# Two constants loaded later, other PSUM banks for the first SwiGLU block, another order of outputs and splits in the S5 layer

## Chip, cores and metric

The kernel runs on one core of a Trainium2 chip. The metric is the device time of one launch, in microseconds (us). Three runs of the kernel before gave 1011.68, 1011.71 and 1012.67 us, median 1011.71. One further run was made with the hardware profiler on: it took 1011.32 us, and its trace spans 1009.5 us from the first instruction to the last. Engine names are those of the profile: PE is TensorE's matmul, PEld its weight load, DVE is VectorE, ACT is ScalarE, POOL is GpSimd, SP is SyncE, whose queue issues most DMAs.

## The reference

A trunk of two layers for 256 tokens of width 1024, all in float32. Each layer adds to the residual `h` half of a SwiGLU of the normalized `h`, then a mixer, then half of a second SwiGLU.

```python
def swiglu(h, w_gate, w_up, w_down):
    return (jax.nn.silu(h @ w_gate) * (h @ w_up)) @ w_down
...
    for layer in range(DEPTH):
        h = h + MACARON_WEIGHT * swiglu(rms_norm(h, ffn_norm[layer, 0]), ffn_w_gate[layer, 0],
                                        ffn_w_up[layer, 0], ffn_w_down[layer, 0])
        hn = rms_norm(h, mix_norm[layer])
...
            h = h + s5_mixer(hn, ...)      # layer 0
            h = h + moba_mixer(hn, ...)    # layer 1
        h = h + MACARON_WEIGHT * swiglu(rms_norm(h, ffn_norm[layer, 1]), ...)
```

The S5 mixer multiplies by `w_in`, runs a diagonal complex state space along the tokens, takes `gelu`, gates with `g * sigmoid(g @ w_glu)` and multiplies by `w_out`. The hidden width of a SwiGLU is 2816.

## The kernel before

**Stages.** Six stages follow one another: f00 (first SwiGLU), s5, f01, f10, moba, f11. The tokens are two tiles t = 0, 1 of 128 rows; `h` stays in SBUF. Nearly every product is made three times as exact as one pass by splitting both operands into a high and a low part: `mm3` issues high x high, high x low and low x high into one PSUM accumulation.

**Weights.** The weights come through one stream (`Stream`, L36). A unit is one DMA'd tile `raw` of 1 MB; there are RAW = 3 such tiles, so the DMA of unit n is issued once unit n - 3 has been split. A unit has two halves. `split` (L72) makes the next half: ACT writes its high part `whi` (L81, or L87 as two pieces where a norm's gain `gT` is multiplied in), DVE writes the low part `wlo` (L82 or L88). There are HB = 9 slots for split halves; `release` gives a slot back after the last matmul on it. Splits are issued in the order of the units, at hand-placed calls of `st.pump()`; what a `pump` finds no slot or no raw tile for is left to a later one, and `get` splits on the spot what is still missing. Since ACT and DVE work in the order in which they were given their instructions, the place of a `pump` decides what stands ahead of a split and behind it.

**PSUM.** Eight banks: two taken in turn by `psM` (products of gate and up, L131), two in turn by `psR` (transposes and small products, L134), four by `psA(i)` (accumulators, L137).

**Start and f00.** ACT's queue issues the identity (L236), the SwiGLUs' norm scales (L252), the mixers' norm scales (L254) and, in `gains` (L274), the mask and the rotary tables; SP's queue issues the first half of x, then the first weights. PE multiplies ones by ones meanwhile (`busy`, L1317). `gains` transposes the scales (L276, L277). `pre` and `parts` bring x into transposed high and low parts, in the `psA` banks. `gu0` (L438) then computes the first block of 256 hidden columns for both token tiles at once, in two `psM` banks; `gated` (L457) takes silu on ACT (L459) into `sg`, issues a pump, and multiplies on DVE (L463). Then comes `gu(1, 0)`, which takes the next `psM` bank. While f00 runs, a generator (`tables`, called from `fill`, L1295) works off the S5 tables; `slot[0]` counts estimated us.

**S5.** `w_in` makes U. For each of 8 blocks b: `t1` (L961) on PE, `rot` (L970) with two scans on DVE and four multiplications on POOL that give `hr`, `y_out` (L1016) with 12 groups of small matmuls into a `psR` bank, gelu on ACT and two transposes `gs` on DVE, `g_tr` (L1036) through another `psR` bank into high and low parts (L1045 on ACT, L1046 on DVE), and `glu` (L1048), 24 matmuls into the four `psA` banks. L1098 to L1103 is the loop for b = 3 to 7: `glu(b-3)`, `y_out(b)`, `t1rot(b+3)`, `g_tr(b-1)`. With the last `glu`, `gate` (L1069) takes a sigmoid on ACT, and on DVE a product (L1074), a cast (L1076) and a difference (L1077) for each pair of blocks; `so` (L1079) multiplies by `w_out`. Pumps stand in `glu` (L1064), and in the loop of `so` over b = 0, 1 and t (L1119, L1120).

**After S5.** `boundary` (L354) does the last two `so` units bank by bank: `finish` (L352, DVE) updates `h`, `prep` (L304) transposes it for the next stage. `ffn_w` (L513) is f01: `gu` with a block of hidden columns on the partitions (L531 to L533), `act` and `dn`.

Of the kernel before, what the change touches and what calls it, by code (L numbers as in the profile page):

```python
# [10 lines left out]
F32 = mybir.dt.float32  # L11
# [104 lines left out]
def trunk_kernel(ctx: ExitStack, tc, x, ffn_norm, ffn_w_gate, ffn_w_up, ffn_w_down, mix_norm,  # L116
                 s5_w_in, s5_a_re, s5_a_im, s5_log_dt, s5_b_re, s5_b_im, s5_c_re, s5_c_im, s5_d,
                 s5_w_glu, s5_w_out, moba_w_qkv, moba_q_norm, moba_k_norm, moba_w_out,
                 consts, out, phases=("f00", "s5", "f01", "f10", "moba", "f11")):
    nc = tc.nc  # L120
    ctx.enter_context(tc.manual_schedule())
    cp = ctx.enter_context(tc.tile_pool(name="const", bufs=1))
# [4 lines left out]
    fp = ctx.enter_context(tc.tile_pool(name="ffn", bufs=2))  # L127
# [3 lines left out]
    def psM():  # L131
        return pp.tile([128, 512], F32, name="pM", tag="M", bufs=2)

    def psR():  # L134
        return pp.tile([128, 512], F32, name="pR", tag="R", bufs=2)

    def psA(i):  # L137
        return pp.tile([128, 512], F32, name=f"pA{i}", tag=f"A{i}", bufs=1)
# [92 lines left out]
    cst = cp.tile([128, 320], F32, name="cst")  # L231
    ident = cst[:, 0:128]
# [1 line left out]
    cosT = cst[:, 256:288].rearrange("p (t f) -> p t f", t=2)  # L234
    sinT = cst[:, 288:320].rearrange("p (t f) -> p t f", t=2)
    nc.scalar.dma_start(ident, consts[:, 0:128])  # L236
    gn = cp.tile([48, 128], F32, name="gn")
    h2 = cp.tile([128, 2, D], F32, name="h2")
    h = [h2[:, t, :] for t in range(2)]

# [5 lines left out]
    def ld_x(n):  # L246
        for s in range(4):
            off, ap = rows(None, s, n)
            nc.sync.dma_start(h2[s * 32:s * 32 + 32, :, n * 512:(n + 1) * 512],
                              bass.AP(tensor=x.tensor, offset=x.offset + off, ap=ap))  # L250

    nc.scalar.dma_start(gn[0:32], ffn_norm.rearrange("l i (k p) -> (l i k) p", p=128))  # L252
    ld_x(0)
    nc.scalar.dma_start(gn[32:48], mix_norm.rearrange("l (k p) -> (l k) p", p=128))  # L254
    warm(AF.Exp)
    ahead.append(lambda: ld_x(1))
    if "s5" in phases:
# [10 lines left out]
    st = Stream(nc, units, rp, hp)  # L268

    gT = cp.tile([128, 48], F32, name="gT")  # L270
    st.gT = gT

    def gains():
        nc.scalar.dma_start(cst[:, 128:320], consts[:, 128:320])  # L274
        ps = psR()
        nc.tensor.transpose(ps[:, 0:48], gn, ident[0:48, 0:48])  # L276
        nc.vector.tensor_copy(gT, ps[:, 0:48])  # L277


    X = {}  # L280
# [131 lines left out]


    def ffn(tag, nxt, hooks, fill):

        V = nc.vector
        acc = [None] * 4
        AT, AC = {}, {}

        def gu(j, t, hooks):  # L420
            us = [where[tag, "g", j, a] for a in range(2)]
            ps = psM()
            ts = slice(t * 128, t * 128 + 128)
            for k in range(8):
                for fn in hooks.get(k, ()):
                    fn()
                fill(0.7)
                wh, wl = st.get(us[k // 4], (k % 4) // 2)
                c = slice((k % 2) * 512, (k % 2) * 512 + 512)
                mm3(ps, X["h"][:, k, ts], X["l"][:, k, ts], wh[:, c], wl[:, c], k == 0, k == 7)  # L430
                if k % 2:
                    if k < 7 and (j, t, k) != (L, 1, 5):
                        st.pump()
                    if t == 1:
                        st.release(us[k // 4], (k % 4) // 2)
            gated(j, t, ps)

        def gu0():  # L438

            us = [where[tag, "g", 0, a] for a in range(2)]  # L440
            pt = [psM() for t in range(2)]
            for q in range(4):
                u = us[q // 2]
                for t in range(2):
                    for f in hooks.get((q, t), ()):
                        f()
                    ts = slice(t * 128, t * 128 + 128)
                    for k in (2 * q, 2 * q + 1):
                        fill(0.7)
                        wh, wl = st.get(u, q % 2)  # L450
                        c = slice((k % 2) * 512, (k % 2) * 512 + 512)
                        mm3(pt[t], X["h"][:, k, ts], X["l"][:, k, ts], wh[:, c], wl[:, c], k == 0, k == 7)
                st.release(u, q % 2)
            for t in range(2):
                gated(0, t, pt[t])

        def gated(j, t, ps):  # L457
            sg = fp.tile([128, 256], F32, name="sg", bufs=1)
            nc.scalar.activation(sg, ps[:, 0:256], AF.Silu, scale=Rr[t])  # L459
            if (j, t) != (L, 1):  # L460
                st.pump()
            AC[t] = fp.tile([128, 256], F32, name="act", bufs=2)
            V.scalar_tensor_tensor(AC[t], ps[:, 256:512], Rr[t], sg, op0=OP.mult, op1=OP.mult)  # L463

        def tr(j, t):
            if t == 0:
                AT[j] = []
                for i, n in enumerate(("ah", "al")):
                    o = AO[2 * i + j % 2]
                    a2 = fp.tile([128, 640], F32R, name=n, bufs=2)  # L470
                    AT[j].append(a2[:, o:o + 512].rearrange("p (f c) -> p f c", c=256))
            ps = psR()
            pv = ps[:, 0:256].rearrange("p (f c) -> p f c", c=128)
            a = AC.pop(t)
            for f in range(2):
                nc.tensor.transpose(pv[:, f, :], a[:, f * 128:(f + 1) * 128], ident)
            ah, al = (x[:, :, t * 128:t * 128 + 128] for x in AT[j])
            nc.scalar.activation(ah, pv, AF.Copy)
            V.tensor_tensor(al, pv, ah.bitcast(F32), op=OP.subtract)

        def dn(j, f):
            u = where[tag, "d", j]
            for t in range(2):
                for n in range(2):
                    if j == 0 and f == 0:
                        acc[2 * t + n] = psA(2 * t + n)
                    bank_mm(acc, t, n, *AT[j], u, [f], j == 0 and f == 0, False)
                    fill(0.7)
                if t == 1:
                    st.release(u, f)  # L490
                st.pump()

        L = NJ - 1
        for j in range(NJ):
            if j == 0:
                gu0()
                continue
            gu(j, 0, {3: [lambda: tr(0, 0)], 6: [lambda: tr(0, 1)]} if j == 1 else {6: [lambda: tr(j - 1, 1)]})
            if j > 1:
                dn(j - 2, 1)  # L500
            gu(j, 1, {6: [lambda: tr(j, 0)]})
            if j:
                dn(j - 1, 0)

        def part(j, f):
            return lambda t, n: bank_mm(acc, t, n, *AT[j], where[tag, "d", j], [f], False, (j, f) == (L, 1))

        boundary(nxt, [part(L - 1, 1), part(L, 0), part(L, 1)], acc, 0.5, lambda: tr(L, 1))
        st.release(where[tag, "d", L - 1], 1)
        for i in range(2):  # L510
            st.release(where[tag, "d", L], i)
# [429 lines left out]
    def s5(nxt, entry):  # L941
# [65 lines left out]
        def t1rot(b):  # L1007
            t1ld(b)
            rot_ld(b)
# [38 lines left out]
        def glu(b, after=None):  # L1048

            u = where["glu", b // 2]  # L1050
            if b == 0:
                for i in range(4):
                    acc[i] = psA(i)
            gh, gl = GT["h"][:, b, :], GT["l"][:, b, :]
            wh, wl = st.get(u, b % 2)
            for o in range(8):
                d = acc[o // 2][:, (o % 2) * 256:(o % 2) * 256 + 256]
                c = slice(o * 128, o * 128 + 128)
                mm(d, wh[:, c], gh, start=b == 0 and o % 2 == 0, stop=False, skip_group_check=True)
                mm(d, wh[:, c], gl, start=False, stop=False, skip_group_check=True)  # L1060
                mm(d, wl[:, c], gh, start=False, stop=b == NB - 1, skip_group_check=True)
                if o == 7:
                    st.release(u, b % 2)
                if o == 3 and b < 7 or o == 7 and b in (5, 6):  # L1064
                    st.pump()
                if after is not None and o % 2 == 1:
                    after(o // 2)
# [28 lines left out]
        t1rot(5)  # L1096
        g_tr(1)
        for b in range(3, NB):  # L1098
            glu(b - 3)
            y_out(b)  # L1100
            if b + 3 < NB:
                t1rot(b + 3)
            g_tr(b - 1)  # L1103
# [8 lines left out]
        for b in range(2):  # L1112
            for t in range(2):
                for n in range(2):
                    so(b, t, n)
                if t == 1:
                    for i in range(2):
                        st.release(where["so", b], i)
                st.pump()  # L1119
            st.pump()  # L1120

        boundary(nxt, [lambda t, n: so(2, t, n), lambda t, n: so(3, t, n, True)], acc, 1.0)
        for b in (2, 3):
# [160 lines left out]
    tab = tables(tabp) if "s5" in phases else iter(())  # L1284
    next(tab, None)
    slot = [0]

    def clock():
        return slot[0]
# [5 lines left out]
    def fill(dt):  # L1295
        slot[0] += dt
        if slot[0] > 9.0:
            next(tab, None)

    def pre(t, n):  # L1300

# [120 lines left out]
```

## Time and profile before

| | us |
|---|---|
| median of 3 runs | 1011.71 |
| profiled run, its own time | 1011.32 |
| span of its trace | 1009.5 |
| f00 ends, s5 starts (first L378 on the s5 weights) | about 226 |
| s5 ends, f01 starts (first L531) | 334.82 |
| DVE busy over the span | 707.0 |
| ACT busy over the span | 574.4 |

A row of the timeline has the start in us, the duration in us, the engine, the source line, the operation, the tiles written and read, and in brackets how long the engine had been idle and what ended that. Matmuls are pipelined, so a record is longer than the distance to the next one. In the table by windows each engine has its busy us and its count of instructions, then follow the TensorE clock that was granted (1.00 is full), the share of the DMA engines and their GB/s. The list of waits names who waited for whom, the us in total, how often, and the longest.

### The profile page before, as it was taken

The numbers are of one execution on the slowest core, as the hardware profiler recorded it, in microseconds if no ns is written. First come the engines' busy times: TensorE is split into PE (matmuls) and PEld (weight loads), VectorE is DVE, ScalarE is ACT, GpSimd is POOL, SyncE is SP. The second block draws the span as 40 slices with busy tenths as digits, with TensorE's granted clock in tenths as the row PEclk, the third lists the DMA queues.
The fourth block names the chain that finished last, engine by engine and source line by source line (L and its number), as shares of the span: only waits on it lengthen the run. The fifth ranks groups of instructions, "written<-read, shape, count | busy, mean of one in ns | idle before, by whom it ended". The sixth has DMA issues, their size and how long they took to land.

```text
span 1009.5 us, 16571 instructions
## 1 busy us (share of the span) xinstructions
PE 993.0 (98%) x6393; PEld 889.0 (88%) x6393; DVE 707.0 (70%) x1144; ACT 574.4 (57%) x1040; POOL 167.3 (17%) x330
## 2 busy tenths in 40 slices
PE   8999999999999999999999999999999999999998
PEld 6788888888997889999989999999888899999997
DVE  4799676857967677666657766666689667766662
ACT  5656778744335656555546555553788655555551
POOL 4981222113740100000000000000342010000000
PEclk9999999999999999999999999999999999999999
DMA  8886776876735467565626665645354456656531
GB/s 258 231 271 225 240 255 216 280 294 234 269 117 196 139 211 248 168 208 168 208 84 209 235 222 169 208 168 172 117 164 139 159 173 210 223 195 208 169 126 42
DMA packets 137535, 197.59 MB, mean 196 GB/s; under 512 B 16288, under 2 KB 109040, under 8 KB 137200
## 3 DMA queue, kind: packets, MB, share of 16 engines
q1 hardware_dynamic: 133088, 183.16, 54.6%
q0 software_dynamic: 3616, 12.66, 3.2%
q8 instruction: 50, 0.82, 0.3%
q10 hardware_dynamic: 752, 0.71, 0.3%
q14 instruction: 29, 0.24, 0.1%
HBM read 182.84 MB, written 13.66 MB: 195 GB/s over the span
## 4 chain that ended last, share of the span: by engine, by line
PE 87%; DVE 5%; issue 3%; POOL 2%; ACT 2%; ACTq 0%; POOLq 0%; DVEq 0%
PE pM L533 12%; PE pM L531 12%; PE pM L532 12%; PE pA L379 9%; PE pA L380 9%; PE pA L378 9%; PE pM L378 5%; PE pM L379 5%; PE pM L380 5%; DVE wlo L82 1%; PE pR L314 1%; POOL qrs L287 1%; PE pR L863 1%; DVE zo L992 1%; PE pR L843 1%
## 5 line engine op out<-in xcount | busy, mean ns | idle before, releaser
L531 PE MATMUL pM<-xa,whi 128*128 128x256 f32 x1056 | 295.7, 280 | 1.9 <-ACT whi L87 1.9
L533 PE MATMUL pM<-xa,wlo 128*128 128x256 f32 x1056 | 294.8, 279 | 0.3 <-DVE wlo L88 0.3
L532 PE MATMUL pM<-xa,whi 128*128 128x256 f32 x1056 | 294.8, 279 | 0.0
L88 DVE SCALAR_TENSOR_TENSOR wlo<-raw,gT,whi 128x512 fp32r<-128x512 f32 x328 | 228.0, 747 | 71.2 <-ACT whi L87 71.1
L82 DVE TENSOR_TENSOR wlo<-raw,whi 128x1024 fp32r<-128x1024 f32 x156 | 193.0, 1252 | 57.5 <-ACT whi L81 56.2
L87 ACT ACTIVATE whi<-raw,gT 128x512 fp32r<-128x512 f32 x328 | 213.5, 711 | 19.1 <-PE pA L380 14.1
L531 PEld LDWEIGHTS pM<-xa,whi 128*128 128x128 f32 x1056 | 198.5, 188 | 4.4 <-ACT whi L87 2.1
L532 PEld LDWEIGHTS pM<-xa,whi 128*128 128x128 f32 x1056 | 198.5, 188 | 2.5
L533 PEld LDWEIGHTS pM<-xa,wlo 128*128 128x128 f32 x1056 | 198.5, 188 | 0.5 <-DVE wlo L88 0.5
L81 ACT ACTIVATE whi<-raw 128x1024 fp32r<-128x1024 f32 x156 | 160.9, 1054 | 21.1 <-DMA raw<-in_ffn_w_up_dram 6.1
L378 PE MATMUL pA<-whi,ah 128*128 128x512 f32 x352 | 138.9, 395 | 0.3 <-ACT whi L81 0.3
L379 PE MATMUL pA<-wlo,ah 128*128 128x512 f32 x352 | 137.8, 391 | 0.8 <-DVE wlo L82 0.8
L380 PE MATMUL pA<-whi,al 128*128 128x512 f32 x352 | 137.7, 391 | 0.0
L378 PE MATMUL pM<-whi,xa 128*128 128x512 f32 x304 | 126.5, 416 | 2.3 <-DVE act L463 1.9
L546 ACT ACTIVATE sg<-gr 128x256 f32<-128x256 f32 x66 | 27.6, 418 | 165.4 <-DVE gr L543 165.4
L379 PE MATMUL pM<-wlo,xa 128*128 128x512 f32 x304 | 119.8, 394 | 1.7 <-DVE wlo L82 1.6
L380 PE MATMUL pM<-whi,xa 128*128 128x512 f32 x304 | 119.7, 394 | 0.0
L329 POOL TENSOR_TENSOR ms<-ss 128x1 f32<-128x1 f32 x10 | 1.9, 194 | 479.5 <-ACT sq L326 479.5
L380 PEld LDWEIGHTS pA<-whi,al 128*128 128x128 f32 x352 | 66.1, 188 | 14.3
L379 PEld LDWEIGHTS pA<-wlo,ah 128*128 128x128 f32 x352 | 66.2, 188 | 12.4 <-DVE wlo L82 1.1
L378 PEld LDWEIGHTS pA<-whi,ah 128*128 128x128 f32 x352 | 66.1, 188 | 12.0 <-ACT whi L81 0.5
L543 DVE TENSOR_TENSOR gr<-pM,rrow 128x512 f32<-128x512 f32 x66 | 45.5, 689 | 39.8 <-PE pM L533 39.7
(248 smaller groups left out, 1264.1 us busy)
## 6 DMA issues: line engine op xcount, KB each, us to landing
raw<-in_ffn_w_down_dram SPq DMA_DIRECT2D x44, 1024.0 KB, 5.1
raw<-in_ffn_w_gate_dram SPq DMA_DIRECT2D x80, 512.0 KB, 3.7
raw<-in_ffn_w_up_dram SPq DMA_DIRECT2D x80, 512.0 KB, 4.9
raw<-in_moba_w_qkv_dram SPq DMA_DIRECT2D x12, 1024.0 KB, 5.1
TB<-dB SPq DMA_DIRECT2D x8, 768.0 KB, 6.4
raw<-in_ffn_w_gate_dram SPq DMA_DIRECT2D x16, 256.0 KB, 4.5
raw<-in_ffn_w_up_dram SPq DMA_DIRECT2D x16, 256.0 KB, 4.7
dB<-tt POOLq DMA_DIRECT2D x16, 256.0 KB, 5.1
```

Source lines behind the costliest of these rows:

```text
L81: nc.scalar.activation(hi, r, AF.Copy)
L82: nc.vector.tensor_tensor(lo, r, hi.bitcast(F32), op=OP.subtract)
L87: nc.scalar.activation(hi[:, c], r[:, c], AF.Identity, scale=g)
L88: nc.vector.scalar_tensor_tensor(lo[:, c], r[:, c], g, hi[:, c].bitcast(F32), op0=OP.mult, op1=OP.subtract)
L378: mm(o, xh, wh, start=start, stop=False)
L379: mm(o, xh, wl, start=False, stop=False)
L380: mm(o, xl, wh, start=False, stop=stop)
L531: mm(o, a, xh, start=k == 0 and i == 0, stop=False, skip_group_check=True)
L532: mm(o, a, xl, start=False, stop=False, skip_group_check=True)
L533: mm(o, b, xh, start=False, stop=k == 7, skip_group_check=True)
L543: V.tensor_tensor(gr, ps.rearrange("p (i c) -> p i c", i=2), Rr["row"][:, None, :].to_broadcast([128, 2, 256]), op=OP.mult)
L546: nc.scalar.activation(sg, gr[:, 0, :], AF.Silu)
```

## The change

- The mixers' norm scales and the second part of the constants (mask, rotary tables) are no longer loaded by ACT's queue at the start. `more_loads` issues both on SP's queue when the count of us passes 30, `more_gains` transposes the mixers' scales when it passes 50. The first transpose has 32 columns and waits for two loads only.
- `gu0` accumulates in `psA(0)` and `psA(2)`. Its two `gated` issue no pump; two pumps follow both. `sg` of f00 takes the two buffers of `gr` in place of one of its own.
- In the S5 loop `y_out(b)` stands ahead of `glu(b-3)`.
- The additional pump at the end of a `glu` stands in blocks 3, 4 and 5, where it stood in 5 and 6. Each t of the `so` loop pumps twice, eight in all; there were six.

```diff
-    nc.scalar.dma_start(gn[0:32], ffn_norm.rearrange("l i (k p) -> (l i k) p", p=128))
+    nc.scalar.dma_start(gn, ffn_norm.rearrange("l i (k p) -> (l i k) p", p=128))
     ld_x(0)
-    nc.scalar.dma_start(gn[32:48], mix_norm.rearrange("l (k p) -> (l k) p", p=128))
...
     def gains():
-        nc.scalar.dma_start(cst[:, 128:320], consts[:, 128:320])
         ps = psR()
-        nc.tensor.transpose(ps[:, 0:48], gn, ident[0:48, 0:48])
-        nc.vector.tensor_copy(gT, ps[:, 0:48])
+        nc.tensor.transpose(ps[:, 0:32], gn, ident[0:32, 0:32])
+        nc.vector.tensor_copy(gT[:, 0:32], ps[:, 0:32])
+
+    def more_loads():
+        nc.sync.dma_start(gm2, mix_norm.rearrange("l (k p) -> (l k) p", p=128))
+        nc.sync.dma_start(cst[:, 128:320], consts[:, 128:320])
+
+    def more_gains():
+        ps = psR()
+        nc.tensor.transpose(ps[:, 0:16], gm2, ident[0:16, 0:16])
+        nc.vector.tensor_copy(gT[:, 32:48], ps[:, 0:16])
...
-            pt = [psM() for t in range(2)]
+            pt = [psA(2 * t) for t in range(2)]
...
-                gated(0, t, pt[t])
-
-        def gated(j, t, ps):
-            sg = fp.tile([128, 256], F32, name="sg", bufs=1)
+                gated(0, t, pt[t], 0)
+            st.pump(2)
+
+        def gated(j, t, ps, pumps=1):
+            sg = fp.tile([128, 512], F32, name="sg", tag="gr", bufs=2)[:, 0:256]
             nc.scalar.activation(sg, ps[:, 0:256], AF.Silu, scale=Rr[t])
             if (j, t) != (L, 1):
-                st.pump()
+                st.pump(pumps)
...
-                if o == 3 and b < 7 or o == 7 and b in (5, 6):
+                if o == 3 and b < 7 or o == 7 and b in (3, 4, 5):
                     st.pump()
...
         for b in range(3, NB):
+            y_out(b)
             glu(b - 3)
-            y_out(b)
...
-                st.pump()
-            st.pump()
+                st.pump(2)
...
+    extra = [(30.0, more_loads), (50.0, more_gains)]
...
         if slot[0] > 9.0:
             next(tab, None)
+        while extra and slot[0] > extra[0][0]:
+            extra.pop(0)[1]()
```

More of the change, by code (lines that the diff above doesn't have):

```diff
@@ L236, in trunk_kernel @@
     nc.scalar.dma_start(ident, consts[:, 0:128])
-    gn = cp.tile([48, 128], F32, name="gn")
+    gn = cp.tile([32, 128], F32, name="gn")
+    gm2 = cp.tile([16, 128], F32, name="gm2")
     h2 = cp.tile([128, 2, D], F32, name="h2")
```

## Prediction

> **What bounds the kernel now.** First the page: the busy shares and the chain that ended last.
>
> ```profile
> PE 993.0 (98%) x6393; PEld 889.0 (88%) x6393; DVE 707.0 (70%) x1144; ACT 574.4 (57%) x1040; POOL 167.3 (17%) x330
> ...
> PE 87%; DVE 5%; issue 3%; POOL 2%; ACT 2%; ACTq 0%; POOLq 0%; DVEq 0%
> ```
>
> PE sets the time. The change removes no matmul, so it can gain only where PE stands still or runs slowly, and the list of PE's waits says where that is.
>
> ```profile
> PE pM L378 <- DVE act L463: 1.9, 1, 1.9
> PE pM L531 <- ACT whi L87: 1.9, 1, 1.9
> ...
> PE pA L379 <- DVE wlo L82: 1.1, 2, 0.8
> PE pA L378 <- DVE xa L1076: 1.0, 1, 1.0
> ```
>
> Each is one or two events of a microsecond or two, and the diff touches what stands around all four. So I took the timeline around each of them, and the order in which the changed program gives each engine its instructions. Idle time in a row understates a stall, since records overlap: I count the distance from one matmul's start to the next, less the usual pace.
>
> **The first block, 24 to 34 us.**
>
> ```profile
> 23.77 1.05 ACT L81 ACTIVATE whi<-raw 128x1024 fp32r<-128x1024 f32 x1
> 24.28 0.40 PE L380 MATMUL pM<-whi,xa 128*128 128x512 f32 x1
> 24.85 1.23 DVE L82 TENSOR_TENSOR wlo<-raw,whi 128x1024 fp32r<-128x1024 f32 x1 [1.82 <-ACT whi L81]
> 26.00 0.47 DVE L463 SCALAR_TENSOR_TENSOR act<-pM,rr,sg 128x256 f32<-128x256 f32 x1
> 26.59 0.47 ACT L459 ACTIVATE sg<-pM,rr 128x256 f32<-128x256 f32 x1 [1.77 <-DVE act L463]
> 26.62 0.47 PE L378 MATMUL pM<-whi,xa 128*128 128x512 f32 x1 [1.94 <-DVE act L463]
> 26.93 0.46 PE L379 MATMUL pM<-wlo,xa 128*128 128x512 f32 x1
> ```
>
> PE ends `gu0` at 24.28 and goes on at 26.62: the bank for `gu(1,0)` is freed by `act`, which stands on DVE behind the split that `gated` had pumped. In the changed program the bank is free. But `gu(1,0)` needs that very split, and it now stands behind both `sg`. The second `sg` cannot start before PE's last product is done (24.28 + 0.40), so about 24.7; it ends at 25.2, `whi` at 26.2, `wlo` at 27.45. PE's first matmul comes at 26.25 rather than 26.62, but the second, which reads `wlo`, at 27.5 rather than 26.93. So the wait is not removed, it is exchanged for one that ends 0.55 us **later**. The clock must be looked at too:
>
> ```profile
> 20.28:23.69 3.41, 3.41 (x16) 2.54 (x15) 1.29 (x3) 1.30 (x3) 2.83 (x11) 1.00 0.67 201
> 23.69:27.10 3.41, 1.47 (x7) 0.94 (x6) 1.62 (x2) 1.64 (x4) 2.81 (x8) 1.00 1.08 252
> 27.10:30.50 3.40, 3.40 (x9) 2.21 (x9) 2.46 (x3) 1.85 (x2) 3.01 (x6) 0.50 0.07 9
> ...
> 337.68:341.10 3.42, 2.00 (x14) 1.80 (x15) 2.89 (x5) 3.42 (x7) 2.75 (x10) 1.00 0.00 0
> ```
>
> After a stretch in which PE was busy for 1.47 of 3.41 us, the clock was half for 3.4 us (9 matmuls in place of 15 or 16, worth up to 1.6 us). In the changed kernel PE is idle from 24.5 to 26.25 and from 26.5 to 27.5, as much as before, so I expect the half clock again. Partly it hides: the later splits follow at 28.7 and 30.0, and PE at half pace meets neither. I take **+0.3**, with bounds of +0.6 (the delay alone) and -1.0 (the delay, and 1.6 gained by full clock).
>
> That `gu0` writes into the banks of `pre` costs nothing: `parts` reads them on DVE ahead of the first `wlo`, for which PE waits anyway. `sg` in two buffers takes away a wait of ACT for DVE, which is not on PE's path here.
>
> The Trainium skill ("TensorE: Matmul & The Clock Gate", section "Why this matters for your kernels") says that throughput doesn't drop as long as PE has no idle gap over about 3 us. The trace disagrees: a gap of 1.94 us was followed by half clock. By the page the changed kernel would keep full clock, and the term would be -1.0.
>
> **The loads at the start.**
>
> ```profile
> 0.98 5.49 PE L1321 MATMUL pR<-ones 128*128 128x128 f32 x24 [0.98 <-POOL ones L224]
> ...
> 6.40 0.34 PE L276 MATMUL pR<-cst,gn 48*128 48x48 f32 x1
> ```
>
> The first transpose follows directly upon the filler (0.98 + 5.49 = 6.47), so PE wouldn't use earlier scales. The first weights may land earlier, as their issues wait for fewer loads, but what follows runs from PE through `pre` and `parts`, not from a DMA. I count 0 (bounds -0.4 and +0.2). The scales' second transpose costs PE a slot like the row at 6.40: **+0.2**. SP issues two more loads, of 8 and 96 KB, ahead of one refill of f00; refills are issued units ahead: 0, at worst +0.5.
>
> **`y_out` ahead of `glu`.**
>
> ```profile
> 267.25 0.36 PE L1059 MATMUL pA<-xa,whi 128*128 128x256 f32 x1
> ...
> 268.12 0.38 DVE L1046 TENSOR_TENSOR xa<-pR,xa 128x256 fp32r<-128x256 f32 x1
> ...
> 268.55 0.38 PE L1060 MATMUL pA<-xa,whi 128*128 128x256 f32 x1 [0.94 <-DVE xa L1046]
> ```
>
> `glu(0)` does one matmul and then waits for the low part of block 0, until 268.55. It looks as if `y_out(3)` could fill that. But it writes into a `psR` bank, and of the two, `g_tr(1)` has just taken one; the other is that of `g_tr(0)`, which is free only when L1046 has read it. So `y_out(3)` waits for the same instruction: gain 0, and the matmul of 267.25 no longer runs in the gap, **+0.1**. The rest of the loop is the same work in another order.
>
> **The pumps at the gate.**
>
> ```profile
> 306.09 1.99 ACT L81 ACTIVATE whi<-raw 128x1024 fp32r<-128x1024 f32 x2
> 307.16 2.36 DVE L82 TENSOR_TENSOR wlo<-raw,whi 128x1024 fp32r<-128x1024 f32 x2 [1.82 <-ACT whi L81]
> 309.31 0.28 PE L1060 MATMUL pA<-xa,whi 128*128 128x256 f32 x1
> 309.44 0.68 DVE L1074 TENSOR_TENSOR gf<-gf,sg 128x512 f32<-128x512 f32 x1
> 310.73 0.47 PE L378 MATMUL pA<-whi,xa 128*128 128x512 f32 x1 [1.02 <-DVE xa L1076]
> ```
>
> The gate's product waits on DVE behind two splits; PE, done at about 309.55, waits for it. With the pump of block 6 gone, one split is left; the product can start at 307.16 + 1.23 = 308.4, and everything behind it comes 1.04 earlier. Less the 0.1 above: **-0.9**. In all there is one pump more ahead of the gate (10 for 9), so both halves of `so(1)` are split before it. That takes away this stall:
>
> ```profile
> 317.21 0.39 PE L378 MATMUL pA<-whi,xa 128*128 128x512 f32 x1
> 317.92 0.37 SPq L170 DMA_DIRECT2D raw<-in_ffn_w_gate_dram  x1
> 317.94 0.50 PE L379 MATMUL pA<-wlo,xa 128*128 128x512 f32 x1 [0.35 <-DVE wlo L82]
> ...
> 321.50 1.34 ACT L87 ACTIVATE whi<-raw,gT 128x512 fp32r<-128x512 f32 x2 [4.16 <-DMA raw<-in_ffn_w_up_dram]
> ...
> 326.89 0.69 DVE L352 SCALAR_TENSOR_TENSOR h<-pA,h 128x512 f32<-128x512 f32 x1 [3.13 <-PE pA L380]
> ```
>
> 317.94 - 317.21 less a pace of 0.23: **-0.5**. The same split freed the raw tile for f01's first weights: their DMA was issued at 317.92, now at about 308.4.
>
> **The eight pumps of `so`.** They make, ahead of the boundary, the last four halves of `so` and four of f01; before it was five and one. That pays here:
>
> ```profile
> 336.31 0.60 PE L314 MATMUL pR<-cst,h 128*128 128x128 f32 x4
> ...
> 338.81 0.38 PE L531 MATMUL pM<-xa,whi 128*128 128x256 f32 x1 [1.91 <-ACT whi L87]
> ...
> 339.60 0.38 PE L533 MATMUL pM<-xa,wlo 128*128 128x256 f32 x1 [0.29 <-DVE wlo L88]
> ...
> 355.21 0.28 PE L533 MATMUL pM<-xa,wlo 128*128 128x256 f32 x1
> 355.75 0.50 PE L378 MATMUL pA<-whi,ah 128*128 128x512 f32 x1 [0.26 <-ACT whi L81]
> 357.01 0.50 PE L379 MATMUL pA<-wlo,ah 128*128 128x512 f32 x1 [0.76 <-DVE wlo L82]
> ```
>
> With the first block's four halves ready, PE goes on after the transposes of 336.31: 2.50 to 338.81, less about 0.4 for them, and 0.4 round 339.60: **-2.5**. ACT and DVE then have two halves fewer to make, and the halves of `dn(0,0)` stand right behind the first `sg` of f01, ready some 4 us ahead of PE. So the pair of stalls at 355 goes: 0.42 + 1.03 = **-1.45**.
>
> What is late next: the last two of f01's halves need its second unit, whose DMA goes out when the second split after the gate is done, about 318.1. The row at 321.50 came 3.6 us after its DMA; so 321.7 for the one and, with a microsecond more of issues, 322.7 for the other; split on DVE by 325.9. `finish` is due at 326.89 - 1.4 = 325.5, behind them on DVE: 0.4 late, and its transposes a full bank's matmuls later: 0 (bound +1).
>
> **Sum**: +0.3 + 0.2 - 0.9 - 0.5 - 2.5 - 1.45 = -4.85, so 4.9 faster. From the profiled run's own 1011.32 (span 1009.5 and 1.8 around it, which I leave as it is) that is 1006.5. The median of the runs is 0.4 above the profiled run, so the forecast is 1006.8 to 1006.9; I put **1006.8**, own range 1005.8 to 1008. The bounds of the single terms added up would give 1003 to 1009; they won't all fall to one side.
>
> **Rivals.**
>
> 1. The boundary holds the gain back. ACT and DVE take their work in order; if f01's second unit lands late, `finish` waits behind its splits, and PE behind `finish`. Against it: the row at 321.50 leaves room. For it: four loads instead of two are in flight, and nothing in the trace shows them at that place. Each us of delay beyond 0.5 is a us lost; with 3 us the time is **1009.3**.
> 2. Full clock in the first block: at 337.68 a stretch with PE busy for 2.00 of 3.42 us kept it, at 23.69 one with 1.47 lost it, and where such stretches begin may shift from run to run. That is 1.3 more than the forecast, **1005.5**. Or `y_out(3)` does fill the gap (if the bank were free): 1.2 more, about the same. Against it: PE is idle for 2.75 of 3 us, and two banks are two.
> 3. Slower: the S5 loop falls behind. `y_out(7)` moves ahead of `glu(4)` and needs `hr(7)` from POOL.
>
> ```profile
> 291.59 1.72 POOL L999 TENSOR_TENSOR hr<-pv,pv 128x256 f32<-128x256 f32 x1
> ...
> 294.90 0.36 PE L1059 MATMUL pA<-xa,whi 128*128 128x256 f32 x1
> ```
>
> `hr(7)` ends at 293.31 and PE comes for it at 294.9: 1.6 us of slack. DVE is nearly full from 268 on, and the changed order puts gelu's transposes ahead of the splits. If each of the four turns from block 3 to block 7 took DVE and POOL t us longer, PE would lose 4t - 1.6; from t = 1.6 on that is more than the 4.85. At t = 2.2 it is 7.2: 1006.8 + 7.2 = **1014**. Against it: the same instructions as before.
> 4. The gain is given back in f01: PE waits again for halves that ACT and DVE cannot make faster. Both have idle time there, and before there is hardly a PE wait behind 357: with most of the 3.95 us of that stage gone, about **1010.5**.
>
> **Chances.** Forecast 0.62; rival 1 0.16, a third of it under 2 us of gain; rival 2 0.14; rival 3 0.05; rival 4 0.03. A measurement tells about 0.2% (2 us) from no change: faster 0.87, same 0.08, slower 0.05. The range from 1004.8 to 1009.2 takes in rival 2 and most of rival 1.
>
> **What would show it.** In the trace after (starts as before unless PE has gained or lost by then): PE's second matmul of `gu(1,0)` waits for `wlo` to about 27.5, with half clock behind it; `y_out(3)` starts only when the low part of block 0 is read out, near 268.5; the gate's stall shrinks from 1.2 to 0.2; no wait of L531 or of the first `dn` in f01; the first load of f01 near 308. Wrong it would be if f01's halves came later than the boundary, or PE waited in blocks 4 to 7 of S5.

## The result and the profile after

The changed kernel took 1009.04 us (median of 9 runs, 1005.99 to 1012.03); the kernel before, run beside it, 1012.67 (9 runs, 1011.41 to 1014.65). The ratio is 0.9958 with a 95% interval of 0.9941 to 0.9976, so some 4.2 us faster (3.6 by the medians) where 4.9 had been forecast.

The runs of the changed kernel fall into two groups, and the granted clock tells them apart: four took 1005.99 to 1006.29 us at a mean clock of 0.999 to 1.000, five took 1009.04 to 1012.03 us at 0.993 to 0.996. The profiled run, 1010.79 us with a span of 1009.0, is of the second kind. So its trace shows what the change gains and also what takes most of it away again. A mean clock of 0.994 over 1009 us stands for some 12 us at half clock; in the trace they are 3.4 us in the first block, 6.8 in S5 and 1.8 at the end, after PE's last matmuls.

From the page of the changed kernel, the busy shares, the chain, and then, from its list of PE's waits (who waits for whom, us in total, times, longest), the rows that matter here:

```profile
PE 996.0 (99%) x6394; PEld 892.6 (88%) x6394; DVE 704.6 (70%) x1145; ACT 574.8 (57%) x1040; POOL 165.3 (16%) x330
...
PE 91%; DVE 3%; issue 2%; POOL 2%; ACT 1%; DMA 0%; SPq 0%; ACTq 0%; POOLq 0%; DVEq 0%
```

```profile
PE pA L387 <- DVE wlo L82: 1.6, 2, 0.8
PE pM L386 <- ACT whi L81: 1.5, 1, 1.5
PE pR L1033 <- issue: 1.1, 1, 1.1
...
PE pM L387 <- DVE wlo L82: 0.9, 2, 0.8
PE pR L322 <- DVE h L360: 0.7, 1, 0.7
```

The lines stand some 9 further down than in the kernel before. All four waits with which the prediction began are gone: `gu(1,0)` for `act`, f01 for `whi`, `so` for the gate's product, `so(1)` and `dn` for `wlo`. (The first row above has the name of the last of them, but it is `gu0`'s own two waits at 11.31 and 18.79 us, which stood under `pM` before `gu0` changed its banks.) In the place of the first stands a wait for `whi` and `wlo`; and there are two new ones: `y_out(3)` (L1033) and the first transposes of the boundary (L322), which wait for `finish`. The 0.9 us for which `glu(0)` waited before are gone too; the wait of `y_out(3)` stands in their place. PE is busy for 3 us more than before, though it does the same work but for one small transpose: its mean clock was 0.994, against 0.998 in the trace of before.

The same matmul in both traces, start before and start after, gives the balance stage by stage:

| matmul | before | after | difference |
|---|---|---|---|
| second product of `gu(1,0)` | 26.93 | 27.46 | +0.53 |
| `act`'s first pair of transposes, the second | 30.54 | 31.09 | +0.55 |
| after the added transpose of the scales | 70.54 | 71.51 | +0.97 |
| `y_out(2)`, first | 262.47 | 263.46 | +0.99 |
| `g_tr(7)`, first | 300.48 | 304.95 | +4.47 |
| `so(0)`, first | 310.73 | 314.05 | +3.32 |
| `so(1)`, the one that had waited | 317.94 | 320.70 | +2.76 |
| boundary, first transposes | 328.05 | 331.51 | +3.46 |
| boundary, last group of transposes | 336.31 | 339.82 | +3.51 |
| f01, the one that had waited for `wlo` | 339.60 | 340.50 | +0.90 |
| `dn(0,0)`, second | 357.01 | 356.50 | -0.51 |

Behind 357 us the difference hardly moves; the spans differ by 0.5. From 300 us on the difference falls by 5.0 us; the loop of S5 had cost 3.5, where the prediction counted 0.1. The table by windows of the changed kernel, cut along the stretches in which its clock was granted (busy us of PE and count of records, clock, share of the DMA engines, GB/s), shows how:

```profile
263.07:266.48 3.41, 3.41 (x33) 1.00 1.00 381
266.48:269.89 3.41, 2.31 (x22) 1.00 1.04 398
269.89:273.31 3.42, 3.42 (x18) 0.50 0.37 129
273.31:276.72 3.41, 3.41 (x18) 0.50 0.41 109
276.72:280.13 3.41, 3.41 (x32) 1.00 0.45 181
```

and PE's timeline there, with the instruction of DVE that reads out the bank:

```profile
266.37 1.90 PE L976 MATMUL pM<-U,TA 128*128 128x64 f32 x16
268.10 0.39 PE L1051 MATMUL pR<-cst,gs 128*128 128x128 f32 x2
269.11 0.38 DVE L1055 TENSOR_TENSOR xa<-pR,xa 128x256 fp32r<-128x256 f32 x1
269.59 0.41 PE L1033 MATMUL pR<-U,TB 128*128 128x64 f32 x2 [1.10 <-issue]
...
270.62 0.64 PE L1033 MATMUL pR<-U,TB 128*128 128x64 f32 x2
...
274.43 0.56 PE L1068 MATMUL pA<-xa,whi 128*128 128x256 f32 x1
```

`y_out(3)` waits as foreseen for the `psR` bank of `g_tr(0)`, 1.1 us: DVE has read it out at 269.49, and PE goes on at 269.59 (the profile itself names no releaser, only "issue"). Before, `glu(0)` with its wide products came right behind such a pause. Now the 24 records of `y_out(3)` with 64 columns each come. In the stretch with the pause PE was busy for 2.31 of 3.41 us, and the clock was halved. In the next PE was busy all the time, with 18 records where 32 or 33 are usual, and the clock stayed at half for one stretch more; it was given back at 276.72, after the 256-column products of `glu(0)` had come at 274.43. Two stretches at half clock are worth up to 3.4 us.

### The profile page after: what moved, and what is told of

Read it like the earlier page. It is cut to its first block, busy times and chain, and to the rows that moved or that the text cites. A ratio compares the mean times of both kernels' runs of the same rounds, so it can differ in the third digit from the quotient of the medians.

```text
span 1009.0 us, 16573 instructions
## 1 busy us (share of the span) xinstructions
PE 996.0 (99%) x6394; PEld 892.6 (88%) x6394; DVE 704.6 (70%) x1145; ACT 574.8 (57%) x1040; POOL 165.3 (16%) x330
## 4 chain that ended last, share of the span: by engine, by line
PE 91%; DVE 3%; issue 2%; POOL 2%; ACT 1%; DMA 0%; SPq 0%; ACTq 0%; POOLq 0%; DVEq 0%
PE pM L541 12%; PE pM L540 12%; PE pM L542 12%; PE pA L387 9%; PE pA L386 9%; PE pA L388 9%; PE pM L386 5%; PE pM L387 5%; PE pM L388 5%; PE pR L322 1%; DVE wlo L82 1%; POOL qrs L295 1%; PE pR L872 1%; PE pR L1035 1%; PE pR L1034 1%
## 5 line engine op out<-in xcount | busy, mean ns | idle before, releaser
L82 DVE TENSOR_TENSOR wlo<-raw,whi 128x1024 fp32r<-128x1024 f32 x156 | 190.7, 1237 | 55.2 <-ACT whi L81 54.0
L386 PE MATMUL pM<-whi,xa 128*128 128x512 f32 x288 | 120.0, 417 | 1.5 <-ACT whi L81 1.5
L387 PE MATMUL pM<-wlo,xa 128*128 128x512 f32 x288 | 113.5, 394 | 0.9 <-DVE wlo L82 0.9
L388 PE MATMUL pM<-whi,xa 128*128 128x512 f32 x288 | 113.5, 394 | 0.0
```

Source lines behind the costliest of these rows:

```text
L82: nc.vector.tensor_tensor(lo, r, hi.bitcast(F32), op=OP.subtract)
L386: mm(o, xh, wh, start=start, stop=False)
L387: mm(o, xh, wl, start=False, stop=False)
L388: mm(o, xl, wh, start=False, stop=stop)
```

## The experiments

The runs were made in several series, each with runs of the kernel before beside it; the ratios are against those. The **theory**: the gain is all in the pumps, and the order of `y_out` loses most of it through the clock, because it puts a pause into a long row of narrow products. The **rivals**: the order costs by itself (DVE, the bank), and half clock is chance; or the gain needs the order.

**The order put back.**

```diff
         for b in range(3, NB):
-            y_out(b)
             glu(b - 3)
+            y_out(b)
```

> The kernel after, with glu(b-3) ahead of y_out(b) again. Theory (clock): y_out ahead of glu puts two y_out, the products of t1 and the transposes in one row, some 12 us without a product of 256 or 512 columns, and a pause of 1.1 us in it; one stretch of 3.41 us in it is then judged too light and the clock is halved for two stretches (6.8 us from 269.9 in the trace of after, worth up to 3.4 us). With the order back no half clock between 255 and 310 us, and no run above 1009; the median falls by 1 to 3 us against after's 1009.0. Rival 1 (order costs by itself, through DVE or the psR bank): the pause merely moves, half clock is chance and stays; times go on spreading from 1006 to 1012. Rival 2 (the order helps as meant): slower than after by about 1 us.

Measured: median 1007.13 us (5 runs, 1005.63 to 1009.81), ratio 0.9953 (0.9940 to 0.9965). The profiled run, 1005.63 us, had full clock as long as PE worked, and its loop of S5 took no longer than before. The theory holds for the trace. The median is 1.9 below 1009.04, as expected, but that alone shows little, since the intervals of the two ratios overlap. One run took 1009.81 at a clock of 0.997, so "no run above 1009" failed. There is no trace of that run; what delayed it stays open.

**The order alone.** The kernel before with the edit above the other way round.

> The kernel before, with y_out(b) ahead of glu(b-3) and nothing else. Theory (clock): runs without half clock in S5 take 0.1 us more than before, runs with it 3 to 3.5 us more; median 1 to 3 us above that of before, and in a trace that has it glu(0) starts some 3.4 us later. Rival 1: +0.1 in all runs, same spread as before. Rival 2 (the order helps): 1 us less.

Measured: median 1014.98 us (11 runs) against 1012.32, ratio 1.0021 (1.0012 to 1.0030): slower by 2 to 3 us. Five runs took 1012.58 to 1013.31 at a clock of 0.997 to 0.998, six took 1014.98 to 1016.33 at 0.993 to 0.995. None of the 15 runs of the kernel before beside it was above 1012.86, so here the order alone made the slower group. It is not the only thing that makes one: of the kernel before, 4 of the 9 runs beside the changed kernel took 1014.5 to 1014.65 us, and 4 of 49 in the series of the experiments took 1014.37 to 1014.75. Of none of these runs, and of none of the six here, is there a trace. The profiled run is of the first group: there the S5 loop cost 0.30 us with the clock at full (the difference goes from -0.47 at 45 us to -0.17 at `g_tr(7)`). In this trace the pause fell across the border of two stretches, and neither was followed by half clock:

```profile
264.07:267.48 3.41, 2.94 (x27) 1.00 1.01 396
267.48:270.89 3.41, 2.78 (x25) 1.00 0.59 240
335.75:339.16 3.41, 1.51 (x11) 1.00 0.00 0
339.16:342.57 3.41, 3.13 (x15) 0.50 0.41 105
```

The last two rows are another find: at the entry of f01, where the kernel before waits for its splits, PE was busy for 1.51 of 3.41 us, and there too half clock followed. In the trace of before the borders fell otherwise, and it did not.

**The pumps alone.**

```diff
-                if o == 3 and b < 7 or o == 7 and b in (5, 6):
+                if o == 3 and b < 7 or o == 7 and b in (3, 4, 5):
...
-                st.pump()
-            st.pump()
+                st.pump(2)
```

> The kernel before, with the other places of the pumps in glu and in the loop of so, and nothing else. Theory: the whole gain is here: -0.9 at the gate, -0.5 at so(1), -2.5 at the first block of f01, -1.45 at its first dn, and +0.7 at the boundary, where the last finish stands on DVE behind a half whose weights land late: together -4.6 to -5.0, so 1006.7 to 1007.1 against 1011.7. Rival: part of it needs the changed order in S5 (the splits come elsewhere): -3 or less.

Measured: median 1005.88 us (5 runs, 1005.69 to 1007.90), ratio 0.9942 (0.9930 to 0.9955). In the trace -1.14 at the gate, -0.54 at `so(1)`, +0.42 at the boundary, -2.56 at the entry of f01 (from -1.34 at 328 to -3.90) and -1.40 at `dn(0,0)`: 5.2 in all, with half clock in the first block as in the trace of before. So the whole gain is here, and it needs nothing of the rest. The median is 3 us below that of the whole change, though the intervals of the two ratios just overlap.

**A pump between, in the first block.** The kernel after with

```diff
-                gated(0, t, pt[t], 0)
-            st.pump(2)
+                gated(0, t, pt[t])
```

> The kernel after, with one pump in each gated of gu0 as before, in place of two behind both; the banks stay those of after. Theory: the loss of 0.54 us in the first block is the split standing behind both sg; with the banks free and the split between, gu(1,0) starts at 24.8 and its second product at 26.1, 1.4 us earlier than in after (27.46): -1.4 us, and -1.6 more where the clock stays full. Rival: act now stands behind the split on DVE, the transposes of act or the later splits are late instead, and no more than 0.5 us is gained.

Measured: median 1007.66 us (5 runs, 1006.04 to 1008.37), ratio 0.9954 (0.9941 to 0.9968). First the timeline of after (ACT, then DVE, then PE), then that of this kernel:

```profile
24.73 0.48 ACT L468 ACTIVATE sg<-pA,rr 128x256 f32<-128x256 f32 x1 [0.84 <-PE pA L388]
25.10 2.94 ACT L81 ACTIVATE whi<-raw 128x1024 fp32r<-128x1024 f32 x3
...
26.18 3.64 DVE L82 TENSOR_TENSOR wlo<-raw,whi 128x1024 fp32r<-128x1024 f32 x3 [0.46 <-ACT whi L81]
...
26.20 0.50 PE L386 MATMUL pM<-whi,xa 128*128 128x512 f32 x1 [1.51 <-ACT whi L81]
27.46 0.74 PE L387 MATMUL pM<-wlo,xa 128*128 128x512 f32 x1 [0.76 <-DVE wlo L82]
```

```profile
24.83 1.23 DVE L82 TENSOR_TENSOR wlo<-raw,whi 128x1024 fp32r<-128x1024 f32 x1 [1.81 <-ACT whi L81]
24.85 0.51 PE L386 MATMUL pM<-whi,xa 128*128 128x512 f32 x1 [0.19 <-ACT whi L81]
...
26.11 0.51 PE L387 MATMUL pM<-wlo,xa 128*128 128x512 f32 x1 [0.76 <-DVE wlo L82]
```

The second product comes 1.35 us earlier than in the changed kernel, as the theory had it, and in this trace the clock stays full behind it; `act`'s transposes come 2.7 us earlier. The free banks were worth something, but only with the split where it had been. In S5 this kernel still has the order of after, and in its trace one stretch at half clock. The pause crosses a border of stretches here too, but with 0.8 us of it in one of them:

```profile
262.62:266.04 3.42, 3.14 (x29) 1.00 0.96 381
266.04:269.45 3.41, 2.59 (x24) 1.00 0.64 255
269.45:272.86 3.41, 3.41 (x18) 0.50 0.73 224
272.86:276.28 3.42, 3.42 (x33) 1.00 0.23 89
```

**The pause filled with wide work.** The kernel after, with products that `glu(0)` overwrites:

```diff
         for b in range(3, NB):
+            if b == 3:
+                fz = psA(0)
+                wh0 = st.get(where["glu", 0], 0)[0]
+                for _ in range(8):
+                    mm(fz[:, 0:256], wh0[:, 0:128], GT["h"][:, 0, :], start=True, stop=True)
             y_out(b)
```

> The kernel after, with eight added products of 256 columns (into a bank that glu(0) overwrites; they change no result) ahead of y_out(3), where PE pauses for 1.10 us. Theory (clock): the pause amid products of 64 columns makes one stretch of 3.41 us too light. Filled with some 0.95 us of wide work, no stretch is light: no half clock between 255 and 300 us, no time added, and the slow runs of after (1009 to 1012, 5 of 9) are gone: median 1006 to 1007.5. Rival (half clock is chance, or comes from the long row of light products as such): half clock in S5 stays in about half the runs, median 1009.

Measured: median 1007.67 us (5 runs, 1005.71 to 1008.33, clocks 0.997 to 0.999), ratio 0.9952 (0.9940 to 0.9964). PE does eight products **more** than the changed kernel and no run is above 1009. Its windows, again along the granted stretches, show half clock in the first block and none around the pause; below them the filler in PE's timeline:

```profile
23.55:26.96 3.41, 1.62 (x6) 1.00 1.09 277
26.96:30.37 3.41, 2.84 (x7) 0.50 0.22 33
262.48:265.89 3.41, 3.41 (x33) 1.00 1.01 365
265.89:269.31 3.42, 3.42 (x31) 1.00 1.02 403
269.31:272.72 3.41, 3.26 (x30) 1.00 0.38 157
```

```profile
268.15 1.19 PE L1112 MATMUL pA<-xa,whi 128*128 128x256 f32 x8
269.49 0.41 PE L1033 MATMUL pR<-U,TB 128*128 128x64 f32 x2
```

**The pause filled with narrow work.** The same place, nine products of 64 columns on `y_out(3)`'s operands.

```diff
+                v3 = TB[3][:, 1024:1536].rearrange("p (q c) -> p q c", c=128)
+                for i in range(9):
+                    mm(fz[:, 0:64], v3[:, i % 4, :], U[:, 12 + i % 4, :, :], start=True, stop=True)
```

> As the kernel with the wide filler, but the pause is filled with nine products of 64 columns, some 1.0 us. Theory A (the pause counts): as with the wide filler, no half clock in S5, median 1006 to 1007.5. Theory B (the row of light products counts, the pause is only a part of it): half clock in S5 stays in some runs, median 1008 to 1010. The stretch would then hold some 28 products of 64 columns in place of 19; in before and after such stretches with 30 or 31 were not followed by half clock, which speaks for A.

Measured: median 1007.37 us (6 runs, 1006.54 to 1008.60, clocks 0.997 to 1.000), ratio 0.9954 (0.9942 to 0.9966); full clock throughout in the trace.

```profile
266.67 2.12 PE L1112 MATMUL pA<-U,TB 128*128 128x64 f32 x18
268.62 0.39 PE L1033 MATMUL pR<-U,TB 128*128 128x64 f32 x2
```

Each product has two records and takes 0.22 us, so the filler was twice as long as meant. In the trace the loop of S5 took 0.97 us more than before, where the order alone had cost 0.30; so the filler cost some 0.7, and without it the median would be about 1006.7, by that estimate. Theory A holds in the trace: narrow work too kept the clock, with no pause in it. It is the pause in a row of narrow products, not the row.

Put side by side, the traces say what the loop of S5 (from `y_out(2)` to `g_tr(7)`) took more than before: nothing with the order put back or with the pumps alone, 0.30 us with the new order and no half clock (the order alone, and the wide filler), 1.83 with one stretch at half clock (the kernel with the pump between), 3.48 with two. The counts of runs are weaker evidence. No run with a filler was above 1009, against 5 of 9 of the changed kernel, but they were made in another series, and beside the changed kernel even the kernel before had more runs above 1014 than elsewhere.

**Parts of the rest alone.** First the kernel before with the whole edit of `gu0` (banks, no pump between, `sg` in two buffers):

> The kernel before, with gu0 in the banks of after and both pumps behind both gated, and nothing else. Theory: the first block alone costs 0.5: second product of gu(1,0) at 27.5 in place of 26.93, so +0.5 in a run whose clock is halved in the first block as in before's trace; some 1.1 less than before where the clock there happens to stay full. Rival: free banks gain something by themselves, -0.4 (first product at 26.2 in place of 26.62).

Measured: 1011.98 us (12 runs), ratio 0.9997 (0.9988 to 1.0005): nothing that can be measured. The second product comes at 27.46 (+0.54), but this run kept full clock there, and `act`'s transposes come 1.03 earlier: 0.5 lost, 1.6 won by the clock. The half clock came at f01 instead:

```profile
25.58:28.99 3.41, 2.03 (x8) 1.00 0.60 58
...
336.19:339.60 3.41, 1.47 (x10) 1.00 0.00 0
339.60:343.01 3.41, 3.41 (x19) 0.50 0.74 244
```

Then the loads alone (the first part of the front's diff and the two entries of `extra`):

> The kernel before, with the later loads and the second transpose of the scales, and nothing else. Theory: +0.2 to +0.4 (a transpose of its own on PE at about 70 us), nothing at the start, where the first transpose still follows upon the filler. Rival: the earlier weights bring the first split and so the first products forward: -0.4 or more.

Measured: 1012.85 us (12 runs), ratio 1.0006 (0.9998 to 1.0015). In the trace +0.36 at the added transpose (from +0.19 to +0.55), whose row is 0.23 us long: a single small transpose costs a slot and delays its neighbours.

**The best of both.** The kernel before with the pumps of after and the banks of after, the pump between `sg` and `act` as before:

```diff
-            pt = [psM() for t in range(2)]
+            pt = [psA(2 * t) for t in range(2)]
...
-            sg = fp.tile([128, 256], F32, name="sg", bufs=1)
+            sg = fp.tile([128, 512], F32, name="sg", tag="gr", bufs=2)[:, 0:256]
```

> The kernel before, with the pumps of after (in glu and in the loop of so), and gu0 in the banks of after but with the pump between sg and act as before; order of y_out and loads as before. Theory: 1005.9 of the kernel with the pumps alone, less 0.8 (second product of gu(1,0) at 26.1 in place of 26.93), less 1.6 where the clock then stays full: 1003.5 to 1005.1, the fastest of all. Rival (the loads matter): it is no faster than 1005.9.

Measured: 1004.24 us (5 runs, 1003.70 to 1004.61, clocks 0.999 and 1.000), ratio 0.9921 (0.9909 to 0.9932). Then one pump fewer, which tries the boundary:

```diff
-                st.pump(2)
+                st.pump(1 if b and t else 2)
```

> As the kernel before this one, with one pump fewer at the end of the loop of so: three halves of f01 split ahead of the boundary in place of four. Theory: the fourth half, whose weights land late, held finish back on DVE (0.4 to 0.7 us of PE's wait at the first transposes of the boundary); without it that wait goes, -0.5; and the fourth half, split behind finish, is in time for the last columns of the first block. Rival: the first block of f01 then waits for it, as L531 did in before: +0.5 or more.

Measured: 1003.36 us (4 runs, 1003.22 to 1003.39), ratio 0.9912 (0.9900 to 0.9925). First ACT and DVE of the changed kernel, then DVE and PE of this one:

```profile
328.68 1.34 ACT L87 ACTIVATE whi<-raw,gT 128x512 fp32r<-128x512 f32 x2 [1.25 <-DMA raw<-in_ffn_w_up_dram]
...
329.44 1.41 DVE L88 SCALAR_TENSOR_TENSOR wlo<-raw,gT,whi 128x512 fp32r<-128x512 f32 x2 [0.84 <-ACT whi L87]
330.77 1.28 DVE L360 SCALAR_TENSOR_TENSOR h<-pA,h 128x512 f32<-128x512 f32 x2
```

```profile
322.86 0.69 DVE L352 SCALAR_TENSOR_TENSOR h<-pA,h 128x512 f32<-128x512 f32 x1 [0.94 <-PE pA L380]
...
324.02 0.60 PE L314 MATMUL pR<-cst,h 128*128 128x128 f32 x4
```

In the changed kernel the fourth half waits for its DMA and `finish` stands behind it, for two banks at once; with three halves `finish` waits for PE alone, PE has no wait at the boundary, and f01 has none for the fourth half. The theory holds, with -0.9: in its trace the kernel with four halves loses 0.95 us at the boundary against the kernel before, this one nothing.

Last, the products of high by high parts of `glu(0)` moved ahead of the others, into the pause of 0.94 us that the kernel before has there:

```diff
+            for o in range(8 if b == 0 else 0):
+                d = acc[o // 2][:, (o % 2) * 256:(o % 2) * 256 + 256]
+                mm(d, wh[:, o * 128:o * 128 + 128], gh, start=o % 2 == 0, stop=False, skip_group_check=True)
             for o in range(8):
...
-                mm(d, wh[:, c], gh, start=b == 0 and o % 2 == 0, stop=False, skip_group_check=True)
+                if b:
+                    mm(d, wh[:, c], gh, start=False, stop=False, skip_group_check=True)
```

> As the fastest kernel so far (pumps of after less one, gu0's banks with the pump between, order of before), and the eight products of high by high parts in glu(0) stand ahead of its others: they fill the pause of 0.94 us before the low part of block 0. Theory: -0.8 to -0.9, so 1002.5, and no half clock in S5. Rival: PE only meets DVE later in S5 and nothing is gained.

Measured: 1002.46 us (4 runs, 1002.41 to 1002.49, clocks 0.999 and 1.000), ratio 0.9900 (0.9886 to 0.9915): the fastest of all, 10 us below the kernel before, and the one whose runs lie closest together. In its trace the loop of S5 took 0.85 us less, with full clock.

```profile
265.00 1.19 PE L1058 MATMUL pA<-xa,whi 128*128 128x256 f32 x8
266.31 0.39 PE L1064 MATMUL pA<-xa,whi 128*128 128x256 f32 x1
```

## Why the prediction was right, and where it was not

The direction was right, and the median lies in the wide range of 1004.8 to 1009.2, though above the narrower one of 1005.8 to 1008. What was predicted of the pumps came to within 0.3 us in each term but `finish`. But the sum of -4.85 is not that of the profiled run, whose terms below add up to -0.5, and that the median came so near is in part luck: it is the lowest of the five runs with the lower clock, and one of these fewer would have made it about 1006.3. The terms:

- **First block** (+0.3): the order of events was as told, `wlo` ready at 27.46 (27.5 forecast); +0.55 where half clock follows, as in both traces, 1.0 faster than before where it does not. The term was +0.55 or -1.0, by what the clock did in the run, and the +0.3 between them is neither.
- **Loads and the second transpose** (+0.2): +0.42 between 30 and 71 us, of which +0.37 at the transpose; +0.36 there in the kernel with the loads alone. The start gained nothing, as forecast.
- **`y_out` ahead of `glu`** (+0.1): the wait was foreseen to the instruction (1.10 us for the bank of `g_tr(0)`), and at full clock the order costs 0.30. The step that failed is "The rest of the loop is the same work in another order": the order decides what stands beside the pause. The term was +3.5 in the profiled run, mis-sized by the clock, which the prediction reckons with in the first block and not here. With the pause filled, none of 11 runs has a clock below 0.997; with the order alone on the kernel before, 6 of 11 runs are 2 to 4 us longer.
- **Gate and `so(1)`** (-0.9 and -0.5): -1.15 and -0.56. The first load of f01 went out at 312.87 in place of 317.92, near the 308.4 forecast plus the 4.5 us lost by then.
- **Entry of f01** (-2.5): -2.61; **its first `dn`** (-1.45): -1.41. Both to about a tenth.
- **Late next, `finish`** (0, bound +1): +0.75. The DMA of f01's second unit was issued later than reckoned (322.37; 318.1 plus the 2.8 us lost by then would be 320.9), and its second part, the fourth half, took longer (6.3 us from there to its split, where 4.6 were reckoned); the split waited for it until 328.68, and `finish` behind it on DVE until 330.77. That is rival 1 in small, and the one pump fewer took it back.

Of the rivals, number 2 (full clock in the first block, 1005.5) is, by their clock, what the four runs at 1006.0 to 1006.3 are, and it is the trace of the kernel with the order put back (1005.63). The forecast case itself, half clock in the first block and none in S5, is met by the trace with the wide filler, whose run took 1007.21: 1006.8 was forecast. The runs of the kernel with the order put back at 1006.8 to 1007.1 (clock 0.997 and 0.998) may be the same case; of them there is no trace. Rival 3 had S5 slower by the engines falling behind: S5 was slower, but PE never waited for `hr` in blocks 4 to 7; it was the clock.

The Trainium skill ("TensorE: Matmul & The Clock Gate", section "What's actually happening") says that the gate watches a free-running window of 3413 ns, that does not start anew with the kernel. The traces agree: while PE works, the half clock comes in stretches of 3.41 us or 6.83, on a grid that stands elsewhere in each run (first border of a half stretch at 27.11 in before, 27.55 in after, 269.45 with the pump between). The Trainium skill says too, in the same section, that the clock falls after an idle window. Here less was enough: stretches with 1.15 to 2.59 us of work in 3.41 were followed by half clock.

## What to carry to other kernels

Where a tuned kernel waits on PE for a microsecond or two, ask first which split, copy or load stands ahead of the awaited one on its engine: here some moved calls of `pump` gave 5.2 us in the trace. Where PE must pause, look at what stands beside the pause and at the granted clock behind it: here a pause of 1.1 us amid narrow products cost 0.3 us at full clock and up to 3.5 where the clock fell. Better still, fill the pause with products that have to be made anyway: that gave 0.85 us here. When runs of one kernel fall into groups, look at each run's clock before comparing medians.

## What the runs showed of the hardware

Each stretch below is one of 3.41 us on the grid of its own trace.

- In these traces the work that kept the clock depended on its kind. With products of 256 and 512 columns, stretches with 1.15 to 1.62 us of busy time were followed by half clock, those with 1.94 to 2.04 were not (but one with 1.57, the last with matmuls in the trace of the order alone, was not either, so the busy time does not settle it by itself). With products of 64 columns for the most part, 2.31 and 2.59 were, 2.78 and 2.94 were not. With 4 products of 256 columns among those of 64, 2.47 was not (the kernel with the order put back), nor 2.48 with 8 of them (the kernel before):

```profile
266.05:269.46 3.41, 2.48 (x21) 1.00 1.03 415
```

- At half clock, a stretch filled with 64-column products (18 records, PE busy for all of it) did not bring full clock back; one with 7 to 9 products of 512 columns did, and so did one with 15 of 256 columns. So half clock can last longer amid narrow work; that is one event in one trace.
- The same kernel meets a different grid in each run. The kernel before has the half clock in the first block in its trace, others of its runs have a clock of 1.000 (1010.84 and 1010.93 us) or of 0.994 (1014.37 to 1014.75 us). Of these last there is no trace; that the pause of `glu(0)` or the entry of f01 is what they met is likely, but was not shown.
